# Down projection of an encoder layer: 12 of 22 inner tiles by seven products instead of eight

## The chip, the cores and the metric

The kernel runs on one core of a Trainium2 chip. The metric is the device time of one execution in microseconds. A core has five engines with instruction streams of their own: TensorE (PE; PEld is its weight load), VectorE (DVE), ScalarE (ACT), GpSimd (POOL) and SyncE (SP, which here only starts DMA transfers). They wait for one another by semaphores.

## The reference

One layer of a hybrid encoder on x of 1 x 1024 x 1024 in float32: two token mixers behind a common input projection, their gated sum, and a feed-forward with a gate that is convolved over three positions. D_FF is 2816, which is 22 tiles of 128.

```python
h = _rmsnorm(x, attn_norm_w[layer])
y = _token_mixers(h, w_in[layer], ...)
x = x + jnp.einsum("bsd,de->bse", y, w_out[layer])
h2 = _rmsnorm(x, ffn_norm_w[layer])
x = x + _conv_glu_ffn(h2, ffn_w_up[layer], ffn_dw_w[layer], ffn_dw_b[layer], ffn_w_down[layer])
...
def _conv_glu_ffn(h, w_up, dw_w, dw_b, w_down):
    up = jnp.einsum("bsd,df->bsf", h, w_up)
    gate, val = jnp.split(up, 2, axis=-1)
    gate = _dwconv_centred(gate, dw_w, dw_b)
    return jnp.einsum("bsf,fd->bsd", jax.nn.silu(gate) * val, w_down)
```

The output is the final RMSNorm of x. The change concerns the last product, with `w_down` (2816 x 1024), which is called the down projection here.

## The kernel before

**Numbers in two parts.** Each float32 operand of a large matrix product is split into a high part, rounded to the format that PE multiplies fast (ACT casts it), and a low part, the operand less its high part (DVE subtracts). `split` (L124) does both; both inputs of the subtraction lie in SBUF. `mm3` (L148 to L150) then makes three matmuls: high by high, high by low, low by high. Activations lie transposed, so an output tile is 128 features by 512 positions, half of the sequence, and fills one bank of PSUM. Weights are the stationary operand.

**Ordinary jobs.** `std_job` loads weights for one output tile (`raw_w`, tile `wr`), splits them into two pages `wp`, and accumulates over its inner tiles, for one half of the sequence and then the other. `run_jobs` prepares the next job's weights while one runs. Every two inner tiles a job yields; such a piece is the clock by which `later` schedules chores (loads, splits, gates).

**Seven products.** `pair_job` makes two output tiles and both halves as one 2 x 2 block product in seven products instead of eight, after Winograd. The order is 1, 2, 6, 7, 5, 4, 3. Products 1, 6, 5 and 3 accumulate on one bank (`row`, tag mm), 7 and 4 on another (`col`, tag sc), 2 on a third (tag tr). After 1, 6 and 7 ACT copies the bank into pages `su` (p1, u2, p7; L376); the evacuations to the quadrants (0,0), (1,1), (1,0) and (0,1) follow products 2, 5, 4 and 3. Product 3 starts on the bank that the evacuation of (1,1) reads. The operands are sums and differences of quadrants: the activations' are made once per stage, the weights' sums for each job. In the feed-forward's up projection (22 jobs, four inner tiles per quadrant, 84 matmuls each) the sums of weights are made by DMA transfers that accumulate (`G.dma_start(..., accum_op=ALU.add)`, L301, issued by GpSimd): the column sum `sw`, then two sums into `wr`, each waiting for the one before. The weights of products 1 and 2 (w1/w2) share pages, as do those of 7 and 5 (w7/w5), and of 6 and 3 (w6/w3); w4 stands alone.

**Feed-forward.** `ffn_job(j)` is such a pair job for tile j of the gate and of the value. Its `evac` keeps the value in `ft` pages (L1504) and the gate in `gp`; `gated` runs as a chore during the next job: convolution on ACT and DVE (L1486, L1488), silu, two multiplications on DVE (L1497, L1498), and the store to `d_g` (L1499), which SP issues.

**Down projection.** It goes over the 22 inner tiles in groups of 4, 4, 5, 5 and 4. For a group, `load_g` fetches the two halves of each inner tile into a landing buffer (`ev` or `tm`, seven together), and splits them into pages `hx` or `gx` (48 together). Eight ordinary jobs, one for each output tile, go over the group; the first group's results are copied to `xr` by ACT (L1633), those of the next three are added by DVE (L1639). While a group runs, the next one's operands are loaded, a half every two pieces. The last group runs half after half, adds the residual, transposes, and normalises (L1674, L1675, L1689 and on).

**What sets the order.** PE's order is the program's. The other engines' orders are planned by a scheduler when the kernel is built, with a cost model of its own, except that instructions given to `pin` keep their order; an engine then runs its instructions strictly in the planned order and stands still at the first one that has to wait.

Of the kernel before, what the change touches and what calls it, by code (L numbers as in the profile page):

```python
# [47 lines left out]
def tile_hybrid_encoder(  # L48
# [109 lines left out]
    def later(n, do):  # L158

        chores.append([n, do])  # L160
# [118 lines left out]

        return prep, run  # L280

    def pair_job(src0, src1, nk, acts, wpool, pool, evac, su=4, first=False, late=False, now=False, direct=False, columns=1):

        def steps(w):  # L290
            def both(src, alt, late=late):
                hi, lo = split(w_page(2 * nk, alt), w_page(2 * nk, alt), src, V, late)
                return [(hi[:, :nk], lo[:, :nk]), (hi[:, nk:], lo[:, nk:])]

            def add(o, a):
                if first:
                    V.tensor_tensor(o, o, a, op=ALU.add)
                elif direct:
                    pin(V.tensor_tensor(o, o, a, op=ALU.add))
                else:  # L300
                    G.dma_start(o, a, accum_op=ALU.add)  # L301
# [8 lines left out]
            nc.sync.dma_start(col[:, nk:], src1[:, :nk])  # L310
            if first:
                other = column_page()
                nc.sync.dma_start(other, src1)
                add(col, other)
            elif not direct:
                add(col, src1)
            def sums():
                add(rows[:, :nk], col[:, nk:])
                add(rows[:, nk:], rows[:, :nk])

            def quadrant():
                a22 = pool.tile([P, nk, P], F32, tag="w4", name=nm("w4"), bufs=1)
                nc.sync.dma_start(a22, src1[:, nk:])
                return a22

            if now:
                w[1], w[2] = both(rows, None, False)
                sums()
                yield 0
                w[6], w[3] = both(rows, None, False)  # L330
                yield 1
                a22 = quadrant()
                yield 2
                w[7], w[5] = both(col, pool)
                yield 4
            elif direct:
                yield 2
                other = raw_w(src1, 2 * nk)
                yield 2
                w[1], w[2] = both(rows, None)  # L340
                a22 = quadrant()
                yield 6
                add(col, other)
                sums()
                yield 1
                w[6], w[3] = both(rows, None)
                yield 1
                w[7], w[5] = both(col, pool)
                yield 4
            else:  # L350
                yield 4
                w[1], w[2] = both(rows, None)
                sums()
                a22 = quadrant()
                yield 6
                w[7], w[5] = both(col, pool)
                yield 3
                w[6], w[3] = both(rows, None)
                yield 3
            one = w_page(2 * nk, pool)  # L360
            w[4] = split(one[:, :nk], one[:, nk:], a22, V, late)

        def prep():
            w = Weights(steps)
            return w if late else w.all()

        def run(w):
            def product(i, acc, fresh=True):
                for k in range(nk):
                    mm3(acc, w[i], acts(i)[k], k, fresh and k == 0, k == nk - 1, not fresh)  # L370
                    if k % 2 == 1 or k == nk - 1:
                        yield

            def copy(acc):
                t = page(pool, "su", su)
                A.copy(t, acc)  # L376
# [128 lines left out]
    d_h2 = scratch("d_h2", ND, 2)  # L505
    d_t4 = scratch("d_t4", ND // 2)
    d_g = scratch("d_g", NF, 2)

    def in_cols(c0):
        return w_cols(w_in, 0, ND, c0)  # L510
# [966 lines left out]

    up, gp = Later(), []

    def ffn_job(j):  # L1480
        val = [None, None]

        def gated(hf):
            o, g = hf * H, gp[j % 2]
# [11 lines left out]
            pin(A.activation(c, c, AF.Silu))  # L1496
            V.tensor_tensor(c, c, rstd2[hf], op=ALU.mult)  # L1497
            V.tensor_tensor(val[hf], val[hf], c, op=ALU.mult)  # L1498
            nc.sync.dma_start(d_g[j][hf], val[hf])  # L1499

        def evac(e, half, x0, x1=None, op=None):
            if e == 1:
                val[half] = page(up, "ft", 8)
                V.tensor_tensor(val[half], x0, x1, op=op)  # L1504
                return
            g = gp[j % 2]
# [15 lines left out]
            up,  # L1522
            evac,
            late=True,
            now=j == 0,
            direct=j in (1, 2),
        )

    s_out = Stream(
# [74 lines left out]
    gs, jobs = [], []  # L1604

    def load_g(f, half):

        t = next(landing)()
        nc.sync.dma_start(t, d_g[f][half])
        while len(gs) <= f:  # L1610
            gs.append([None, None])

        def parts():
            gs[f][half] = split(g_page(), g_page(), t, V, True)

        return parts

    s_ffn.fill(14 * (NF - 1) - s_ffn.count)
    for f in range(groups[0]):
        for half in range(2):  # L1620
            later(4, load_g(f, half))
            s_ffn.fill(1)
# [4 lines left out]

    fd = tc.alloc_tile_pool(name="fd", bufs=1, reuse_waits="tile")
    xr = [[page(fd, "xr", 2 * ND) for _ in range(2)] for _ in range(ND)]

    def first_evac(i):
        def f(half, acc):
# [10 lines left out]
    def down_jobs(f0, n, evac):  # L1643
        return [
            std_job(
                w_cols(ffn_w_down, f0 * P, n, i * P), n, lambda k, half: gs[f0 + k][half], evac(i)
            )
            for i in range(ND)
        ]

    def last_jobs(f0, evac):
# [3 lines left out]
        def job(i, half):  # L1655
# [4 lines left out]
                    kept[i] = split(*pages, raw, V)  # L1660
                return kept[i]

            return prep, std_job(None, 4, lambda k, h: gs[f0 + k][h], evac(i), (half,), 1)[1]

        return [job(i, half) for half in range(2) for i in range(ND)]

# [13 lines left out]
    def turn_out(i, half):  # L1680

        t = xr[i][half]
        if i == 0:
            out_sum.append(fd.tile([P, ND, 4], F32, tag="os", name=nm("os"), bufs=2))
            out_y.append(fd.tile([P, 4, D], F32, tag="y", name=nm("y"), bufs=2))
        ss, y = out_sum[half], out_y[half]
        b = bank(next(y_tags))
        for c in range(4):
            T.transpose(b[:, c * P : (c + 1) * P], t[:, c * P : (c + 1) * P], ident)  # L1689
        for c in range(4):  # L1690
            junk = fd.tile([P, P], F32, tag="oj", name=nm("oj"), bufs=2)
            A.activation(
                junk, b[:, c * P : (c + 1) * P], AF.Square, accum_out=ss[:, i, c : c + 1]
            )
        if i == ND - 1:
            rs = cp.tile([P, 4], F32, name=nm("frs"), tag="frs", bufs=2)
# [20 lines left out]
    def scale_out(half, c):  # L1717
# [9 lines left out]
        n = half * 4 + c  # L1727
        nc.sync.dma_start(out[0, n * P : (n + 1) * P, :], y[:, c, :])

    out_sum, out_y, out_r = [], [], []  # L1730
    fnw = fd.tile([P, D], F32, name="fnw")
    f0 = 0
    nc.sync.dma_start(
        fnw, bass.AP(tensor=final_norm_w.tensor, offset=final_norm_w.offset, ap=[[0, P], [1, D]])
    )
    for n, group in enumerate(groups):
        last = n == len(groups) - 1
        if last:
            st = Stream(run_jobs(last_jobs(f0, final_evac)))
            st.fill(4 * ND + 3)  # L1740
            finish(0)
            st.drain()
            advance_chores(1 << 10)
            finish(1)
        else:
            st = Stream(run_jobs(down_jobs(f0, group, add_evac if n else first_evac)))
            st.fill(12)
            for f in range(f0 + group, f0 + group + groups[n + 1]):
                for half in range(2):
                    later(4, load_g(f, half))  # L1750
                    st.fill(2)
            st.drain()
            advance_chores(1 << 10)
        f0 += group
    fd.release()


# [30 lines left out]
```

## Time and profile before

| | |
|---|---|
| median of three runs | 1769.15 us (1767.91 to 1770.44) |
| profiled execution | 1768.21 us, span 1766.4 |
| mean granted PE clock | 0.996 |
| PE busy | 1728.3 us (98%) |
| DVE busy | 1206.5 us (68%) |
| ACT busy | 808.0 us (46%) |
| POOL busy | 158.4 us (9%) |

The span runs from the first to the last instruction of the profiled execution; the time also holds what lies around it. A row of a group of instructions gives line, engine, operation, output and inputs by name, shape and count, then busy time and mean duration in ns, then the idle time before them and what ended it. Rows of the timeline begin with the start and the duration in us. PE's matmuls overlap, so the mean duration of one is longer than the step from one to the next. The feed-forward lies roughly from 1080 to 1510 us of the span, the down projection from there to the end.

### The profile page before, as it was taken

The numbers are of one execution on the slowest core, as the hardware profiler recorded it, in microseconds if no ns is written. First come the engines' busy times: TensorE is split into PE (matmuls) and PEld (weight loads), VectorE is DVE, ScalarE is ACT, GpSimd is POOL, SyncE is SP. The second block draws the span as 40 slices with busy tenths as digits, with TensorE's granted clock in tenths as the row PEclk, the third lists the DMA queues.
The fourth block names the chain that finished last, engine by engine and source line by source line (L and its number), as shares of the span: only waits on it lengthen the run. The fifth ranks groups of instructions, "written<-read, shape, count | busy, mean of one in ns | idle before, by whom it ended". The sixth has DMA issues, their size and how long they took to land.

```text
span 1766.4 us, 30281 instructions
## 1 busy us (share of the span) xinstructions
PE 1728.3 (98%) x11878; PEld 1422.8 (81%) x11878; DVE 1206.5 (68%) x1839; ACT 808.0 (46%) x1518; POOL 158.4 (9%) x171
## 2 busy tenths in 40 slices
PE   8999999999999999999999999999999999999997
PEld 6878888887888787888878888788888888888885
DVE  5599999646688877887365667666676667444455
ACT  7444443334576666776541345333444344422223
POOL 2201111100000000000000002111111111000000
PEclk9999999999999999999999999999999999999998
DMA  8777878856653443435487665677677766534233
GB/s 286 242 166 187 198 176 212 200 143 198 205 184 106 122 123 109 135 113 192 127 259 212 194 207 170 144 161 155 143 146 153 149 138 149 157 103 125 74 92 137
DMA packets 331061, 286.56 MB, mean 162 GB/s; under 512 B 24222, under 2 KB 251302, under 8 KB 330918
## 3 DMA queue, kind: packets, MB, share of 16 engines
q1 hardware_dynamic: 277878, 248.96, 45.2%
q0 software_dynamic: 43824, 34.61, 13.7%
q10 hardware_dynamic: 9216, 1.05, 0.4%
q8 instruction: 93, 1.52, 0.4%
q14 instruction: 50, 0.41, 0.1%
HBM read 189.40 MB, written 76.81 MB: 151 GB/s over the span
## 4 chain that ended last, share of the span: by engine, by line
PE 82%; ACT 5%; DVE 4%; DMA 4%; issue 3%; POOL 1%; ACTq 0%; SPq 0%; POOLq 0%; DVEq 0%
PE mm L148 19%; PE mm L150 19%; PE mm L149 19%; PE sc L148 4%; PE sc L150 4%; PE sc L149 4%; PE ob L1286 2%; PE tr L148 2%; PE tr L150 2%; PE tr L149 2%; PE sc L1113 1%; DMA tm<-d_bm 1%; POOL ors L520 1%; PE sc L1196 1%; DMA sw<-in_ffn_w_up_dram 1%
## 5 line engine op out<-in xcount | busy, mean ns | idle before, releaser
L148 PE MATMUL mm<-hx,wp 128*128 128x512 f32 x1144 | 457.5, 400 | 6.1 <-ACT su L376 2.9
L150 PE MATMUL mm<-hx,wp 128*128 128x512 f32 x1144 | 447.3, 391 | 1.6 <-DVE wp L124 1.6
L149 PE MATMUL mm<-hx,wp 128*128 128x512 f32 x1144 | 446.5, 390 | 0.0
L124 ACT CAST wp<-wr 128x1024 fp32r<-128x1024 f32 (+2 forms) x171 | 162.2, 949 | 341.4 <-PE mm L149 225.5
L148 PEld LDWEIGHTS mm<-hx,wp 128*128 128x128 f32 x1144 | 215.0, 188 | 53.0 <-ACT su L376 3.3
L150 PEld LDWEIGHTS mm<-hx,wp 128*128 128x128 f32 x1144 | 215.0, 188 | 49.8 <-DVE wp L124 3.9
L149 PEld LDWEIGHTS mm<-hx,wp 128*128 128x128 f32 x1144 | 215.4, 188 | 42.2 <-issue 0.7
L124 DVE TENSOR_TENSOR wp<-wr,wp 128x1024 fp32r<-128x1024 f32 (+2 forms) x169 | 186.7, 1105 | 83.0 <-ACT wp L124 78.8
L966 DVE SCALAR_TENSOR_TENSOR acc<-gl,v_b,acc 128x1024 f32<-128x1024 f32 x120 | 150.5, 1306 | 0.4
L1639 DVE TENSOR_TENSOR xr<-mm,xr 128x512 f32<-128x512 f32 x48 | 33.2, 692 | 72.4 <-PE mm L150 72.4
L1062 DVE TENSOR_TENSOR qF<-qF,tb 128x512 f32<-128x512 f32 x96 | 65.4, 689 | 15.5 <-ACT A L1094 14.0
L376 ACT COPY su<-mm 128x512 f32<-128x512 f32 x82 | 47.6, 581 | 61.3 <-PE mm L150 61.1
L124 ACT CAST wq<-sw 128x1024 fp32r<-128x1024 f32 x41 | 43.1, 1051 | 61.7 <-PE mm L149 40.3
L1062 DVE TENSOR_TENSOR kG<-kG,tb 128x512 f32<-128x512 f32 x96 | 65.9, 689 | 5.1 <-PE sc L1196 4.8
L1488 DVE SCALAR_TENSOR_TENSOR tm<-gp,v_a,tm 128x512 f32<-128x512 f32 x88 | 66.1, 751 | 1.9
L148 PE MATMUL mm<-hy,wp 128*128 128x512 f32 x164 | 64.5, 393 | 0.0
L148 PE MATMUL tr<-hx,wp 128*128 128x512 f32 x164 | 64.3, 392 | 0.0
L148 PE MATMUL sc<-hy,wq 128*128 128x512 f32 x164 | 64.2, 392 | 0.0
L149 PE MATMUL mm<-hy,wp 128*128 128x512 f32 x164 | 64.2, 392 | 0.0
L150 PE MATMUL sc<-hy,wq 128*128 128x512 f32 x164 | 64.2, 391 | 0.0
L150 PE MATMUL tr<-hx,wp 128*128 128x512 f32 x164 | 63.8, 389 | 0.0
L149 PE MATMUL tr<-hx,wp 128*128 128x512 f32 x164 | 63.8, 389 | 0.0
(356 smaller groups left out, 3424.2 us busy)
## 6 DMA issues: line engine op xcount, KB each, us to landing
wr<-in_w_in_dram SPq DMA_DIRECT2D x48, 512.0 KB, 5.1
wr<-in_ffn_w_up_dram SPq DMA_DIRECT2D x24, 512.0 KB, 4.0
sw<-in_ffn_w_up_dram SPq DMA_DIRECT2D x44, 256.0 KB, 3.2
d_g<-ft SPq DMA_DIRECT2D x44, 256.0 KB, 3.2
sw<-in_ffn_w_up_dram POOLq DMA_DIRECT2D x20, 512.0 KB, 8.5
sw<-in_w_in_dram SPq DMA_DIRECT2D x38, 256.0 KB
wr<-sw POOLq DMA_DIRECT2D x33, 256.0 KB, 3.4
wr<-wr POOLq DMA_DIRECT2D x33, 256.0 KB, 3.5
```

Source lines behind the costliest of these rows:

```text
L124: parts = A.copy(hi, src), eng.tensor_tensor(lo, src, hi.bitcast(F32), op=ALU.subtract)
L148: T.matmul(acc, whi[:, k, :], ahi, start=first, stop=False, skip_group_check=again)
L149: T.matmul(acc, whi[:, k, :], alo, start=False, stop=False, skip_group_check=again)
L150: T.matmul(acc, wlo[:, k, :], ahi, start=False, stop=last, skip_group_check=again)
L376: A.copy(t, acc)
L520: hold(G.tensor_tensor(dst, dst, mhalf.to_broadcast(list(dst.shape)), op=ALU.pow))
L966: V.scalar_tensor_tensor(acc, g[:, k : k + S], tap(k), acc, op0=ALU.mult, op1=ALU.add)
L1062: V.tensor_tensor(o, a, b, op=op)
L1113: T.matmul(b[g, o], A_t[:, at : at + 32], Q_t(at), start=True, stop=True)
L1286: T.matmul(o[:, sl], l, r, start=(n == 0), stop=(n == len(terms) - 1))
L1488: V.scalar_tensor_tensor(c, g[:, o + k : o + k + H], vec("fdw", k * NF + j), c, op0=ALU.mult, op1=ALU.add,)
L1639: V.tensor_tensor(xr[i][half], acc, xr[i][half], op=ALU.add)
```

## The change

Twelve inner tiles, 6 to 17, go through the down projection as two groups of six by `pair_job`: three inner tiles per quadrant, output tiles i and i + 4 as a pair, four jobs of 63 matmuls per group. Tiles 0 to 5 form one ordinary group before them, 18 to 21 the last group, as before. Three things go with it.

- The operands. The feed-forward takes tiles 6 to 17 in pairs (f, f + 3). After the gate of the second tile of a pair, `g_sums` makes three differences and one sum on DVE, out of `ft` pages, and SP stores them to `d_gc`. One half of the first tile of each pair is no longer stored, as nothing reads it. `load_seven` fetches and splits 21 operand tiles per group into the same 48 pages: 12 for the first seven-product group while the ordinary group runs, 9 when its pages come free; for the second group three early and 18 around the last job of the first.
- The weights. `pair_job` gets a third way of making sums (`sums_on`): two plain loads, `sr` and `so`, two buffers each; w1/w2 split from `sr`; then four additions on GpSimd, two into `sw` and two in place into `sr`; then the splits of w7/w5, w6/w3 and w4.
- The evacuations. `seven_evac` adds to `xr`: for three of four quadrants GpSimd first adds `xr` to, or subtracts it from, the SBUF page (p1, u2, p7), and DVE combines that with the bank; the fourth is one DVE addition.

In the planned order GpSimd does for each pair job: the addition to p1, the four sums for the next job, and among or after the last of them the additions to u2 and p7.

The pools are laid out anew: `fs` holds the new stage's tiles (`sr`, `so`, `sw`, `wq`, `su`), and the output pages `y` come after it in `fy`. Up to the end of the feed-forward, each engine's planned order is that of before but for the new subtractions and stores.

```diff
+            if sums_on is not None:
+                rows, other = (
+                    wpool.tile([P, 2 * nk, P], F32, tag=tag, name=nm(tag), bufs=2)
+                    for tag in ("sr", "so")
+                )
+                nc.sync.dma_start(rows, src0)
+                nc.sync.dma_start(other, src1)
+                r0, r1, o0, o1 = rows[:, :nk], rows[:, nk:], other[:, :nk], other[:, nk:]
+                yield 4
+                w[1], w[2] = both(rows, None)
+                col = wpool.tile([P, 2 * nk, P], F32, tag="sw", name=nm("sw"), bufs=columns)
+                for o, a, b in (
+                    (col[:, :nk], r0, o0), (col[:, nk:], o0, o1), (r0, r0, col[:, nk:]), (r1, r1, r0)
+                ):
+                    pin(sums_on.tensor_tensor(o, a, b, op=ALU.add))
+                yield 6
+                w[7], w[5] = both(col, pool)
+                yield 3
+                w[6], w[3] = both(rows, None)
+                yield 3
+                one = w_page(2 * nk, pool)
+                w[4] = split(one[:, :nk], one[:, nk:], o1, V, late)
+                return
...
+    def g_sums(f, b11, b12, b21, b22):
+        def less(a, b):
+            o = page(up, "ft", 8)
+            V.tensor_tensor(o, a, b, op=ALU.subtract)
+            return o
+
+        t7 = less(b12, b22)
+        nc.sync.dma_start(d_gc[f][3], t7)
+        t6 = less(t7, b11)
+        nc.sync.dma_start(d_gc[f][2], t6)
+        t5 = less(b11, b12)
+        nc.sync.dma_start(d_gc[f][1], t5)
+        t4 = page(up, "ft", 8)
+        V.tensor_tensor(t4, t6, b21, op=ALU.add)
+        nc.sync.dma_start(d_gc[f][0], t4)
...
-            nc.sync.dma_start(d_g[j][hf], val[hf])
+            if not (hf and j in b12_only):
+                nc.sync.dma_start(d_g[j][hf], val[hf])
+            if hf and FIRST <= j < LAST0:
+                kept_g.append((j, *val))
+                if len(kept_g) == 2:
+                    (f, b11, b12), (_, b21, b22) = kept_g
+                    kept_g.clear()
+                    g_sums(f, b11, b12, b21, b22)
...
-    groups = [4, 4, 5, 5, 4]
+    def load_seven(f0, i, k):
+        f = f0 + k
+        src = {1: d_g[f][0], 2: d_g[f + NS][0], 3: d_g[f + NS][1]}
+        return load_part((f0, i, k), src[i] if i < 4 else d_gc[f][i - 4])
...
-    def add_evac(i):
-        def f(half, acc):
-            V.tensor_tensor(xr[i][half], acc, xr[i][half], op=ALU.add)
+    def seven_evac(i):
+        def f(e, half, x0, x1=None, op=None):
+            t = xr[i + e * ND // 2][half]
+            if x1 is None:
+                V.tensor_tensor(t, x0, t, op=ALU.add)
+                return
+            if (e, half) == (1, 1):
+                G.tensor_tensor(x0, x0, t, op=ALU.add)
+            else:
+                G.tensor_tensor(x1, x1, t, op=op)
+            V.tensor_tensor(t, x0, x1, op=op)
...
+    for s in range(SEVENS):
+        todo = [(FIRST + 2 * NS * s, i, k) for i in PRODUCTS for k in range(NS)]
+        if s == 0:
+            at = [12 + 2 * n for n in range(12)] + [starts[0] - 2 + n for n in range(9)]
...
+            at = [starts[s] - 36 + 6 * n for n in range(NS)]
+            at += [
+                starts[s] - per_seven - 2 + per_seven // 7 * n + max(0, k - 1)
+                for n in range(1, 7)
+                for k in range(NS)
+            ]
+        for n, key in zip(at, todo):
+            fill_to(n)
+            later(4, load_seven(*key))
```

More of the change, by code (lines that the diff above doesn't have):

```diff
@@ L280, in duo_job, with pair_job @@
         return prep, run
-    def pair_job(src0, src1, nk, acts, wpool, pool, evac, su=4, first=False, late=False, now=False, direct=False, columns=1):
+    def pair_job(src0, src1, nk, acts, wpool, pool, evac, su=4, first=False, late=False, now=False, direct=False, columns=1, sums_on=None):
         def steps(w):
@@ L1600, in g_page, with load_part, parts @@
         return hx() if next(n_g) == 0 else page(fd, "gx", 16, F32R)
-    groups = [4, 4, 5, 5, 4]
     landing = itertools.cycle([ev] * 3 + [tmp] * 4)
-    gs, jobs = [], []
-    def load_g(f, half):
[L1608 to L1616, printed above, removed]
+    gs = {}
+    def load_part(key, src):
+        t = next(landing)()
+        nc.sync.dma_start(t, src)
+        def parts():
+            gs[key] = split(g_page(), g_page(), t, V, True)
+        return parts
+    def load_g(f, half):
+        return load_part((f, half), d_g[f][half])
+    def load_seven(f0, i, k):
+        f = f0 + k
+        src = {1: d_g[f][0], 2: d_g[f + NS][0], 3: d_g[f + NS][1]}
+        return load_part((f0, i, k), src[i] if i < 4 else d_gc[f][i - 4])
     s_ffn.fill(14 * (NF - 1) - s_ffn.count)
-    for f in range(groups[0]):
+    for f in range(FIRST):
         for half in range(2):
@@ L1728, in scale_out @@
         nc.sync.dma_start(out[0, n * P : (n + 1) * P, :], y[:, c, :])
[L1730 to L1744, printed above, removed]
-        else:
[L1746 to L1754, printed above, removed]
+    out_y, out_r = [], []
@@ new lines, in tile_hybrid_encoder, with fill_to @@
+    per_std, per_seven = 2 * ((FIRST + 1) // 2), 7 * ((NS + 1) // 2)
+    jobs = std_down(0, FIRST, first_evac)
+    first_seven = seven_down(FIRST)[0]
+    starts = [ND * per_std]
+    for s in range(SEVENS):
+        jobs += seven_down(FIRST + 2 * NS * s)
+        if s == 0:
+            jobs[ND] = (lambda: ahead[0], first_seven[1])
+        starts.append(starts[-1] + ND // 2 * per_seven)
+    st = Stream(run_jobs(jobs, 1))
+    ahead = [None]
+    def fill_to(n):
+        while st.count < n:
+            st.fill(1)
+            if st.count == starts[0] - 2 * per_std + 2:
+                ahead[0] = first_seven[0]()
+            elif ahead[0] is not None and st.count < starts[0] - per_std + 2:
+                ahead[0].tick()
@@ L1755, in tile_hybrid_encoder @@
+    n = starts[-1] - per_seven - 12
+    for f in range(LAST0, NF):
+        for half in range(2):
+            fill_to(n)
+            later(4, load_g(f, half))
+            n += 3
+    st.drain()
+    advance_chores(1 << 10)
+    fs.release()
+    fy = tc.alloc_tile_pool(name="fy", bufs=1, reuse_waits="tile")
+    st = Stream(run_jobs(last_jobs(LAST0, final_evac)))
+    st.fill(4 * ND + 3)
+    finish(0)
+    st.drain()
+    advance_chores(1 << 10)
+    finish(1)
+    fy.release()
     fd.release()
```

58 lines of the change are left out of this document (45 added, 13 removed).

## The prediction

> **What bounds the kernel now.** I read the page first, then a table by stretches, then who waited for whom on PE, then the down projection and one feed-forward job in time.
>
> ```profile
> span 1766.4 us, 30281 instructions
> PE 1728.3 (98%) x11878; PEld 1422.8 (81%) x11878; DVE 1206.5 (68%) x1839; ACT 808.0 (46%) x1518; POOL 158.4 (9%) x171
> ...
> 1170.00:1400.00 230.00, 230.00 (x1004) 188.22 (x1003) 156.17 (x204) 93.61 (x132) 39.36 (x36) 1.00 0.70 149
> 1520.00:1700.00 180.00, 180.00 (x796) 149.10 (x795) 80.01 (x120) 48.05 (x82) 0.00 (x0) 1.00 0.34 103
> ...
> PE mm L150 <- DVE wp L124: 1.6, 3, 0.6
> ```
>
> The two middle lines are a stretch of the feed-forward and one of the down projection (length, then busy time and count of PE, PEld, DVE, ACT, POOL, then granted clock, DMA share, GB/s). PE never rests in either, so a matmul taken away is time gained, but at its pace and not at the 390 ns that the page gives for one: 180/796 = 0.226 us in the down projection, 230/1004 = 0.229 in the feed-forward. DVE has room in the down projection (80 of 180 us) and little in the feed-forward (156 of 230). GpSimd does nothing at all in the down projection. The last line says that in the whole run PE waited for split weights three times, 1.6 us together: what feeds it comes in time, so every later feed has to be looked at against its margin.
>
> **What goes.** Twelve inner tiles cost 12 x 8 outputs x 2 halves x 3 = 576 matmuls; as two groups of seven products they cost 2 x 4 x 7 x 3 x 3 = 504. The built program has 72 fewer: 72 x 0.226 = **-16.3 us**.
>
> **Pace of the products.** The other seven-product stage at hand, the feed-forward, runs at 0.229. At that pace the 504 matmuls lose 504 x 0.003 = 1.5 us, at the pace of the down projection nothing. I take **+0.5**, bounds 0 and 1.5.
>
> **Feed-forward: four more subtractions in six jobs.** In the built order the four stand on DVE directly ahead of the evacuation of quadrant (1,1), after the last multiply of the gate; product 3 accumulates on the bank which that evacuation reads.
>
> ```profile
> 1398.39 0.69 DVE L1511 TENSOR_TENSOR gp<-gp,rs 128x512 f32<-128x512 f32 x1
> 1398.99 0.69 DVE L1498 TENSOR_TENSOR ft<-ft,tm 128x512 f32<-128x512 f32 x1
> 1399.60 1.22 DVE L124 TENSOR_TENSOR wp<-wr,wp 128x1024 fp32r<-128x1024 f32 x1
> ...
> 1403.86 0.69 DVE L1498 TENSOR_TENSOR ft<-ft,tm 128x512 f32<-128x512 f32 x1
> 1404.30 0.39 PE L150 MATMUL mm<-hx,wq 128*128 128x512 f32 x1
> 1404.73 0.69 DVE L1504 TENSOR_TENSOR ft<-su,mm 128x512 f32<-128x512 f32 x1 [0.17 <-PE mm L150]
> 1407.29 0.39 PE L148 MATMUL mm<-hy,wp 128*128 128x512 f32 x1
> ...
> 1424.64 0.69 DVE L1498 TENSOR_TENSOR ft<-ft,tm 128x512 f32<-128x512 f32 x1
> 1425.25 0.68 DVE L1504 TENSOR_TENSOR ft<-su,mm 128x512 f32<-128x512 f32 x1
> 1426.83 0.39 PE L148 MATMUL mm<-hy,wp 128*128 128x512 f32 x1
> ```
>
> One after the other, such instructions follow at 0.61 us (first three lines). So the evacuation starts no sooner than 1404.55 + 4 x 0.61 = 1406.99, ends at 1407.68, and product 3, which began at 1407.29, begins some 0.45 later. In the next job the evacuation began at 1425.25; 2.44 later it would end at 1428.4, 1.6 after product 3 was due (1426.83). I take 0.6 each: **+3.6**, bounds 2.7 and 10.
>
> The weights' sums of the feed-forward are a chain of transfers, and its slack is gone in some jobs:
>
> ```profile
> d_g<-ft SPq DMA_DIRECT2D x44, 256.0 KB, 3.2
> sw<-in_ffn_w_up_dram POOLq DMA_DIRECT2D x20, 512.0 KB, 8.5
> ...
> 1408.63 0.50 SPq L310 DMA_DIRECT2D sw<-in_ffn_w_up_dram  x1
> ...
> 1414.27 1.56 POOL L301 DMA_DIRECT2D sw<-in_ffn_w_up_dram  x1 [5.06 <-DMA sw<-in_ffn_w_up_dram]
> ...
> 1413.67 1.05 ACT L124 CAST wp<-wr 128x1024 fp32r<-128x1024 f32 x1 [8.08 <-DMA wr<-wr]
> ...
> 1414.75 1.23 DVE L124 TENSOR_TENSOR wp<-wr,wp 128x1024 fp32r<-128x1024 f32 x1 [3.83 <-ACT wp L124]
> ```
>
> The four new stores (256 KB each) stand on SP ahead of the next loads of sw, and these also wait for the split that now follows the delayed evacuation: 2 us later, behind 1 MB, of which the stretch above moves 149 GB/s on average. The split at 1414.75 is w6/w3, needed from about 1415.5, so a chain that is later by some us shows on PE. I take 0.3 for each of six jobs, **+2.0** rounded up, bounds 0 and 9.
>
> **The new stage: GpSimd and DVE share a way to memory.** No row has a 384-wide GpSimd addition, but nearby ones price it:
>
> ```profile
> 41.36 1.28 POOL L124 TENSOR_TENSOR hx<-ev,hx 128x512 fp32r<-128x512 f32 x1 [9.98 <-ACT hx L124]
> 42.02 0.69 DVE L784 TENSOR_TENSOR gl<-mm,tm 128x512 f32<-128x512 f32 x1 [1.39 <-PE mm L150]
> ...
> 49.58 1.22 DVE L124 TENSOR_TENSOR wp<-wr,wp 128x1024 fp32r<-128x1024 f32 x1
> 50.40 1.55 POOL L124 TENSOR_TENSOR hx<-ev,hx 128x512 fp32r<-128x512 f32 x1 [1.99 <-ACT hx L124]
> ...
> 1084.22 1.04 POOL L548 TENSOR_TENSOR tm<-ident,r 128x512 f32<-128x512 f32 x1
> 1084.46 1.95 DVE L124 TENSOR_TENSOR hy<-ft,hy 128x512 fp32r<-128x512 f32 x2 [1.22 <-ACT hy L124]
> ...
> L124 DVE TENSOR_TENSOR wp<-wr,wp 128x640 fp32r<-128x640 f32 x16 | 13.1, 817 | 0.0
> L124 DVE TENSOR_TENSOR hx<-tm,hx 128x512 fp32r<-128x512 f32 x18 | 12.0, 687 | 4.1 <-ACT hx L124 4.1
> L376 ACT COPY su<-mm 128x512 f32<-128x512 f32 x24 | 13.8, 576 | 16.5 <-PE mm L150 16.5
> L124 ACT CAST wp<-wr 128x640 fp32r<-128x640 f32 x16 | 11.7, 732 | 78.1 <-PE mm L149 78.1
> L124 ACT CAST hx<-tm 128x512 fp32r<-128x512 f32 x18 | 10.5, 617 | 2.1 <-DMA tm<-d_g 2.1
> ```
>
> A GpSimd addition of 512 columns takes 1.28 us, and a DVE instruction with one operand in PSUM runs beside it undisturbed (first two lines). A DVE split, both of whose inputs lie in SBUF, does not: the addition at 50.40 ends at 51.95, 1.15 after the split that ended at 50.80; and the two splits at 1084.46 end at 1086.41, so the first ended at 1085.80, 0.54 after GpSimd's end at 1085.26. They take turns, and the one that waited has all but some 0.15 us still to do. Scaled by columns: an addition of 384 takes 1.0 alone and 0.87 after a wait; a split of 768 takes 0.95 and 0.8, of 384 0.56 and 0.41, of 512 0.69 and 0.54. A DVE evacuation costs 0.69, a copy on ACT 0.58, and a reader of PE starts 0.04 after the last matmul's end (1404.30 + 0.39 to 1404.73).
>
> A pair job has 63 matmuls, products of 2.04 us, 14.3 in all. In the built order GpSimd does in each: the addition to p1, four sums for the next job, the additions to u2 and to p7; only then can DVE evacuate (1,1), on which product 3 waits, due at 12.24. By itself DVE has 3 x 0.95 + 0.56 + 4 x 0.69 = 6.2 us per job and ACT less, so it is the order that costs. A quiet job, from its first matmul: p1 is copied at 2.25 to 2.83 and added by 4.2; w4's split, ready at 3.3, waits and ends at 4.6; sum 1 at 5.5; the split of w1/w2 6.3 (sum 3 overwrites what it reads); sums 2, 3, 4 at 7.2, 8.2, 9.2; u2 10.5; p7 11.8; evacuation 12.5: product 3 is 0.3 late. Each operand split that stands in between adds about 0.45. Five jobs lie between the changes of group: two have one such split, one two, one none, and the last has no sums to make: 4 x 0.3 + 4 x 0.45 = **+3.0**, bounds 0 and 10.
>
> The changes of group. At the first (standard to seven), six of nine operand splits and w6/w3's stand ahead of that evacuation. From 2.9 on the shared way has to carry additions 1.28 + 2 x 1.15, sums 4 x 0.87, splits 6 x 0.54 + 0.8 + 0.8 + 0.41 = 12.3; the evacuation ends at 15.2 + 0.7 = 15.9 instead of 12.2: **+3.7**. At the second, 18 operand pairs are split within two jobs, eight of them ahead of the evacuation: 1.28 + 2.3 + 3.5 + 0.41 + 0.8 + 8 x 0.57 = 12.8, so its end is at 16.4: +4.2, and the next job begins at 18.5. Behind it stand seven operand splits, two evacuations and two splits of weights, the last of them w6/w3: 9 x 0.61 + 0.87 + 0.95 = 7.3 after 16.4, and the next job's first addition and one or two sums (1.2 to 2.6) between: 24.9 to 26.3, where product 6 is due at 22.6: +3.0; its own evacuation adds 0.5. Together **+7.7**. Bounds for both, 3 (at the second ACT casts w6/w3 behind p1's copy and an operand: 2.83 + 0.62 + 0.85, then DVE's 0.95, makes 5.2 against 4.08) and 18. The third change has no sums, and eight pairs over two jobs: 0.
>
> That both inputs in SBUF make the turns, the Trainium skill has as a rule too ("SBUF — State Buffer", section "Who interferes with whom"), but there the one that comes second stands still for the whole of the other and then has all of its own to do. The rows have 0.15 us less, the sum goes by the rows, and what the rule would make of it is rival three.
>
> **What is hidden.** The first group's 12 operand pairs (8 before) take DVE 12 x 0.61 = 7.3 us behind the last feed-forward job; by the built order the twelfth is ready when the first standard job, 36 matmuls or 8.1 us long, reaches it, and the standard jobs' DVE is then more than half idle, as in the stretch from 1520. Operand loads, two a job and more at the changes, find seven landing buffers and 34% of DMA in use there. Each of these, uncovered, would cost its 0.61 per pair or its transfer time once.
>
> **Sum.** -16.3 + 0.5 + 3.6 + 2.0 + 3.0 + 3.7 + 7.7 = +4.2. The profiled execution took 1768.2 (span 1766.4 and 1.8 around it), 0.9 under the median of the runs, 1769.15. So 1772.4 for such an execution, and **1773.3** against the median: what PE saves is given back at hand-overs.
>
> **Rivals.**
> One, faster: the turns rarely meet. If DVE, which can run ahead, has its splits done while GpSimd waits for copies, p7's addition ends by 11.4 in a job and product 3 never waits; that is the point where it turns. For it speaks the pair at 41.36 and 42.02, against it the built order, which puts the sums between p1's and p7's additions in every job. Then the stage costs 0.5 + 2.5 (ACT's order), the feed-forward 3.6 + 1: -16.3 + 0.5 + 3.0 + 4.6 = -8.2, so 1761. Chance 0.25.
> Two, slower: the feed-forward's chain of sums is late by 2 us in all six jobs behind the stores, 10 more than I took: 1783. For it, the split at 1414.75; against it, the job between two such jobs can catch up. Chance 0.15.
> Three, slower: the one that waits has its whole 1.28 or 0.69 still to do, 0.14 more at every hand-over, some 15 at each of two changes of group and 9 in each of five jobs: 75 x 0.14 = 10.5 more, 1784. Against it, the 1.15 and 0.54 above. Chance 0.08. (This is the rule of the Trainium skill's "SBUF — State Buffer" as it is written.)
> That PE's work does not shrink is ruled out by the built order.
>
> **How the numbers follow.** A run can tell about 0.2%, 3.5 us, from no change: 1765.6 to 1772.7. The forecast has 0.52, of which I put 0.05 below that band, 0.18 in it, 0.29 above; its own range is 1766 to 1781. Rival one gives 0.20 faster and 0.05 same, the others 0.23 slower. Faster 0.25, same 0.23, slower 0.52. The range from 1760 to 1785 takes in rivals one to three at their own values and leaves out what lies beyond: the high ends of all bounds at once.
>
> **What would show it.** PE's waits in the new stage name ACT wp/DVE wp (w6/w3) and, at product 3, the evacuation; POOL additions between splits show 1.4 to 1.9 us instead of 1.28. In the feed-forward, six jobs have a gap of 0.4 to 1.7 before product 3. I am wrong if the span from the first pair job to the last is near 8 x 14.3 = 114 us (then rival one), or if the feed-forward lengthens by over 10 us (two).

## The result and the profile after

The changed kernel takes **1776.22 us** (median of 5 runs, 1773.60 to 1779.20) against 1769.15 before: a ratio of **1.0043, interval 1.0029 to 1.0057**. It is slower, by 7 us; 1773.3 was forecast, with a range of 1760 to 1785. The profiled execution took 1773.6 us, the shortest of the five and 5.4 more than the one of before.

First the page of the changed kernel:

```profile
span 1771.8 us, 30408 instructions
PE 1720.7 (97%) x11806; PEld 1410.2 (80%) x11806; DVE 1254.6 (71%) x1873; ACT 839.9 (47%) x1568; POOL 233.8 (13%) x227
```

PE has 72 matmuls less and is busy 7.6 us less, and yet the span is 5.4 us longer. Next its table by stretches: length, then busy time and count of PE, PEld, DVE, ACT, POOL, then granted clock, DMA share, GB/s.

```profile
1509.00:1575.00 66.00, 66.00 (x293) 54.66 (x292) 25.92 (x34) 25.74 (x44) 4.46 (x4) 1.00 0.52 154
1575.00:1590.70 15.70, 13.09 (x54) 9.27 (x52) 13.31 (x13) 9.33 (x17) 9.96 (x7) 1.00 0.47 137
1590.70:1635.00 44.30, 43.09 (x188) 35.01 (x189) 29.77 (x33) 19.37 (x32) 25.68 (x20) 1.00 0.39 113
1635.00:1660.00 25.00, 19.38 (x69) 14.78 (x68) 20.68 (x25) 10.38 (x17) 12.75 (x9) 0.86 0.65 188
...
1640.00:1643.80 3.80, 3.80 (x11) 3.00 (x10) 3.80 (x7) 0.64 (x2) 0.00 (x0) 0.55 0.85 272
```

The six standard tiles (first line) run without a rest, as the whole stage did before. PE rests from the first change of group on: 2.6 us in the second line, 1.2 in the third, 5.6 in the fourth. The fourth has something else: its clock is 0.86, and 0.55 in the last line, a part of it in which PE is always busy and yet has only 11 matmuls in 3.8 us.

Who waited for whom on PE (total, times, longest):

```profile
PE mm L148 <- DVE xr L1716: 7.0, 6, 4.0
...
PE mm L148 <- DVE ft L1562: 2.9, 6, 0.7
PE mm L150 <- DVE wp L124: 2.8, 4, 1.6
...
PE tr L1781 <- DVE xr L1768: 1.6, 2, 0.9
...
PE sc L149 <- DVE hx L124: 1.4, 2, 0.7
```

All but the third row are new. The first is product 3 of the pair jobs waiting for the evacuation of quadrant (1,1), the second the same in the feed-forward, the third split weights (1.6 before), the fourth the end of the kernel, the last the split operands of product 4 at the first change of group.

One feed-forward job in time, where the differences stand ahead of that evacuation:

```profile
1405.09 2.02 DVE L1517 TENSOR_TENSOR ft<-ft,ft 128x512 f32<-128x512 f32 x3
...
1407.03 0.68 DVE L1527 TENSOR_TENSOR ft<-ft,ft 128x512 f32<-128x512 f32 x1
...
1407.56 0.39 PE L150 MATMUL sc<-hy,wq 128*128 128x512 f32 x1
1407.63 0.68 DVE L1562 TENSOR_TENSOR ft<-su,mm 128x512 f32<-128x512 f32 x1
...
1408.36 0.50 PE L148 MATMUL mm<-hy,wp 128*128 128x512 f32 x1 [0.41 <-DVE ft L1562]
```

Product 4's last matmul starts at 1407.56, and the next should follow 0.23 later; it comes at 1408.36, behind the evacuation: 0.57 beyond the step. The six such jobs have 0.85, 0.58, 0.73, 0.58, 0.57 and 0.58.

A quiet pair job, in which GpSimd's queue is the late one:

```profile
1613.50 1.73 POOL L317 TENSOR_TENSOR sw<-so 128x384 f32<-128x384 f32 x1
...
1615.31 1.01 POOL L317 TENSOR_TENSOR sr<-sr,sw 128x384 f32<-128x384 f32 x1
1615.52 1.35 DVE L124 TENSOR_TENSOR hx<-ev,hx 128x512 fp32r<-128x512 f32 x1 [1.16 <-ACT hx L124]
1616.40 1.35 POOL L317 TENSOR_TENSOR sr<-sr 128x384 f32<-128x384 f32 x1
1617.71 1.29 POOL L1715 TENSOR_TENSOR su<-su,xr 128x512 f32<-128x512 f32 x1
1618.97 1.28 POOL L1713 TENSOR_TENSOR su<-su,xr 128x512 f32<-128x512 f32 x1
1620.28 0.69 DVE L1716 TENSOR_TENSOR xr<-su,mm 128x512 f32<-128x512 f32 x1 [3.41 <-POOL su L1713]
...
1621.03 0.50 PE L148 MATMUL mm<-hx,wp 128*128 128x512 f32 x1 [0.56 <-DVE xr L1716]
```

The turns are there: a sum of 384 columns takes 1.01 alone and 1.35 or 1.73 with a DVE split at its side, a split of 512 takes 1.35 instead of 0.69. DVE itself is idle for 3.41 us ahead of the evacuation: it waits for p7's addition, the last of GpSimd's seven instructions in a job.

The second change of group, on PE, DVE and GpSimd:

```profile
1633.49 3.19 DVE L124 TENSOR_TENSOR gx<-tm,gx 128x512 fp32r<-128x512 f32 x2
1634.69 1.44 POOL L317 TENSOR_TENSOR sr<-sr 128x384 f32<-128x384 f32 x1
...
1635.21 0.39 PE L150 MATMUL sc<-hx,wq 128*128 128x512 f32 x1
...
1636.09 1.71 POOL L1713 TENSOR_TENSOR su<-su,xr 128x512 f32<-128x512 f32 x1
1636.61 2.35 DVE L124 TENSOR_TENSOR gx<-ev,gx 128x512 fp32r<-128x512 f32 x2
1638.88 0.67 DVE L1716 TENSOR_TENSOR xr<-su,mm 128x512 f32<-128x512 f32 x1
...
1639.61 0.50 PE L148 MATMUL mm<-hx,wp 128*128 128x512 f32 x1 [4.01 <-DVE xr L1716]
...
1640.58 0.63 PE L148 MATMUL mm<-hx,wp 128*128 128x512 f32 x1
1641.01 0.63 PE L149 MATMUL mm<-hx,wp 128*128 128x512 f32 x1
...
1649.87 0.50 PE L150 MATMUL mm<-hx,wp 128*128 128x512 f32 x1 [1.61 <-DVE wp L124]
```

Splits and additions in turns, then the evacuation, and product 3 is 4.17 us late. One microsecond after PE goes on, its matmuls follow at 0.43 instead of 0.227, eight times. A second pause, for w6/w3, is 1.78 long and is followed by eight more such steps.

### The profile page after: what moved, and what is told of

It is laid out like the page before. It is cut to its first block, busy times and chain, and to the rows that moved or that the text cites. A ratio compares the mean times of both kernels' runs of the same rounds, so it can differ in the third digit from the quotient of the medians.

```text
span 1771.8 us, 30408 instructions
## 1 busy us (share of the span) xinstructions
PE 1720.7 (97%) x11806; PEld 1410.2 (80%) x11806; DVE 1254.6 (71%) x1873; ACT 839.9 (47%) x1568; POOL 233.8 (13%) x227
## 3 DMA queue, kind: packets, MB, share of 16 engines
q10 hardware_dynamic: 9216, 1.05, 0.4%
## 4 chain that ended last, share of the span: by engine, by line
PE 68%; DMA 8%; DVE 7%; ACT 6%; issue 6%; POOL 4%; ACTq 0%; SPq 0%; POOLq 0%; DVEq 0%
PE mm L148 16%; PE mm L149 15%; PE mm L150 15%; PE sc L148 3%; PE sc L150 3%; PE sc L149 3%; DMA sw<-in_ffn_w_up_dram 3%; PE ob L1311 2%; PE tr L150 2%; PE tr L148 2%; PE tr L149 2%; DMA wr<-wr 1%; PE sc L1138 1%; DVE wp L124 1%; POOL sr L317 1%
## 5 line engine op out<-in xcount | busy, mean ns | idle before, releaser
L148 PE MATMUL mm<-hx,wp 128*128 128x512 f32 x1068 | 429.6, 402 | 12.3 <-DVE xr L1716 7.0
L150 PE MATMUL mm<-hx,wp 128*128 128x512 f32 x1068 | 418.7, 392 | 2.5 <-DVE wp L124 2.4
L149 PE MATMUL mm<-hx,wp 128*128 128x512 f32 x1068 | 417.6, 391 | 0.0
L148 PEld LDWEIGHTS mm<-hx,wp 128*128 128x128 f32 x1068 | 201.4, 189 | 58.5 <-DVE xr L1716 8.6
L150 PEld LDWEIGHTS mm<-hx,wp 128*128 128x128 f32 x1068 | 201.1, 188 | 48.2 <-DVE wp L124 4.9
L149 PEld LDWEIGHTS mm<-hx,wp 128*128 128x128 f32 x1068 | 201.7, 189 | 39.5 <-issue 0.7
L124 DVE TENSOR_TENSOR wp<-wr,wp 128x1024 fp32r<-128x1024 f32 (+2 forms) x145 | 169.8, 1171 | 83.7 <-ACT wp L124 73.6
L124 ACT CAST wq<-sw 128x1024 fp32r<-128x1024 f32 (+1 forms) x49 | 49.8, 1016 | 67.2 <-PE mm L149 41.9
L301 POOL DMA_DIRECT2D wr<-sw x33 | 29.2, 885 | 340.2 <-DVE wp L124 203.4
L148 PE MATMUL tr<-hx,wp 128*128 128x512 f32 x180 | 70.5, 392 | 0.0
L150 PE MATMUL tr<-hx,wp 128*128 128x512 f32 x180 | 70.1, 389 | 0.0
L149 PE MATMUL tr<-hx,wp 128*128 128x512 f32 x180 | 70.0, 389 | 0.0
L148 PE MATMUL mm<-hy,wp 128*128 128x512 f32 x164 | 65.1, 397 | 2.9 <-DVE ft L1562 2.9
L400 ACT COPY su<-sc 128x512 f32<-128x512 f32 x49 | 28.9, 589 | 79.6 <-PE sc L150 79.6
L124 DVE TENSOR_TENSOR wq<-sw,wq 128x1024 fp32r<-128x1024 f32 (+1 forms) x49 | 57.9, 1182 | 11.7 <-ACT wq L124 11.4
L148 PE MATMUL sc<-hy,wq 128*128 128x512 f32 x164 | 64.2, 392 | 0.0
```

What stands on the lines that cost most here:

```text
L124: parts = A.copy(hi, src), eng.tensor_tensor(lo, src, hi.bitcast(F32), op=ALU.subtract)
L148: T.matmul(acc, whi[:, k, :], ahi, start=first, stop=False, skip_group_check=again)
L149: T.matmul(acc, whi[:, k, :], alo, start=False, stop=False, skip_group_check=again)
L150: T.matmul(acc, wlo[:, k, :], ahi, start=False, stop=last, skip_group_check=again)
```

## The experiments

Each is compared with runs of the kernel before on its own chip. "Gain" is the ratio of the change (1.0043) less that of the experiment, times 1768 us. The ratios have intervals of 0.0009 to 0.0014 either way, so a gain is uncertain by some 3 us (an estimate from the two intervals). A trace is of one execution only, which can lie some us from the median.

**1. Bank first.** DVE adds the bank to the residual at once, and GpSimd adds the other page afterwards, so that no GpSimd work stands ahead of the evacuation.

```
-                G.tensor_tensor(x0, x0, t, op=ALU.add)
+                V.tensor_tensor(t, t, x1, op=op)
+                G.tensor_tensor(t, t, x0, op=ALU.add)
...
-                G.tensor_tensor(x1, x1, t, op=op)
-            V.tensor_tensor(t, x0, x1, op=op)
+                V.tensor_tensor(t, x0, t, op=ALU.add)
+                G.tensor_tensor(t, t, x1, op=op)
```

> DVE evacuates the bank into xr at once, and GpSimd adds the page (p1, u2, p7) to xr afterwards; the count of operations is that of the change. If PE's waits in the new stage come from DVE standing before quadrant (1,1) for GpSimd's last addition, and from splits and additions taking turns: the quiet jobs lose their 0.4 to 1.2 us ahead of product 3 altogether, the first change of group falls from 3.9 to about 2.2, the first wait of the second from 4.2 to about 2.6 (its eight operand splits still take turns with sums) and, if the half pace after it comes from the length of the pause, that goes too: together about 9 us under the change, near 1767. If instead DVE's own load at the changes of group is what PE waits for, only the quiet jobs gain, 3 us: 1773.

Measured: 1769.89, ratio 1.0009 (0.9999 to 1.0018), a gain of 6.0. A quiet job now, on DVE and GpSimd:

```profile
1619.36 1.01 POOL L317 TENSOR_TENSOR sr<-sr,sw 128x384 f32<-128x384 f32 x1
1620.25 0.69 DVE L1713 TENSOR_TENSOR xr<-xr,mm 128x512 f32<-128x512 f32 x1 [1.84 <-PE mm L150]
1620.44 1.01 POOL L317 TENSOR_TENSOR sr<-sr 128x384 f32<-128x384 f32 x1
```

The evacuation (L1713 here) waits for PE alone, with GpSimd's sums still running, and the pauses of the quiet jobs are gone. Who waited for that evacuation:

```profile
PE mm L148 <- DVE xr L1713: 3.4, 2, 2.8
```

Two waits instead of six, and nearly all of it is at the second change, a pause of 2.96 us. The place of GpSimd's additions ahead of the evacuation is what the quiet jobs paid for. The gain lies between the two expectations, 1767 and 1773: the pause at the second change fell less than expected (to 2.96, where 2.6 was expected), and six half-pace steps still follow it.

**2. Late differences.** The four differences of the feed-forward go six steps later, behind the evacuation.

```
-                    g_sums(f, b11, b12, b21, b22)
+                    later(6, lambda: g_sums(f, b11, b12, b21, b22))
```

> The four subtractions of a pair are called one piece after quadrant (1,1) is evacuated instead of directly ahead of it; nothing else. If the six gaps ahead of product 3 in the feed-forward (0.57 to 0.85 us each) come from that place in DVE's order, they go, and the feed-forward shortens by 4 us: near 1772. If they come from DVE being full in the feed-forward as a whole, the wait moves to another product or to the splits of weights (w6/w3), and the time stays near 1776.

Measured: 1772.58, ratio 1.0023 (1.0009 to 1.0036), a gain of 3.5. The row of waits on L1562 is gone, and the six pauses with it (3.9 us). In their place product 6 starts late three times (0.95, 0.62 and 0.39), which the trace puts down to ACT's copy of p1. That copy stands behind the cast of w6/w3, which waits for the chain of sums: part of what the rival expected. At the first change of group the pauses are those of the changed kernel, but here eight half-pace steps follow them. The waits in the pair jobs are as they were:

```profile
PE mm L148 <- DVE xr L1716: 7.1, 6, 4.0
```

**3. Sums that only write.** Each of the four sums of weights is left out, and two fills with zero stand in its place.

```
-                    pin(sums_on.tensor_tensor(o, a, b, op=ALU.add))
+                    pin(sums_on.memset(o, 0.0))
+                    pin(sums_on.memset(o, 0.0))
```

> Leaves out the weights' sums: each of GpSimd's four sums becomes two fills with zero of the same page, so that GpSimd has about as much to do, in the same places and behind the same waits on DVE's split, but reads nothing. If GpSimd's reads and DVE's splits of two SBUF inputs exclude one another: the splits beside them take their own 0.69 and 0.95 us, product 3 is on time in the quiet jobs, and the first wait of the second change falls from 4.2 to under 1.5 us. If GpSimd is simply late because of what it waits for, and the long rows (1.3 to 1.7 us) come from elsewhere, product 3 is as late as in the change.

Measured, in one run: 1764.11, where the runs of the kernel before on that chip had a median of 1767.87. Of the waits on product 3:

```profile
PE mm L148 <- DVE xr L1717: 2.0, 2, 1.4
```

(L1717 is L1716, one line down.) The quiet jobs have no pause, the first change 0.54 and 0.76, the second 1.52 and 1.38 and no half pace. A split beside the fills takes its own time:

```profile
1599.33 0.42 POOL L317 MEMSET sw<- 128x384 f32 x1
...
1599.49 0.94 DVE L124 TENSOR_TENSOR wp<-sr,wp 128x768 fp32r<-128x768 f32 x1
```

In the changed kernel the same split took 1.17 beside a sum. So GpSimd instructions that only write make no turns here. One run can't give an interval, but the places of the pauses say what the sums cost, in time and in turns together: most of the 7.0. The two can't be told apart here, since the two fills also take less than a sum, 0.84 from one pair to the next against 1.01.

**4. Sums on DVE.**

```
-                sums_on=G,
+                sums_on=V,
```

> The four sums of weights are made by DVE instead of GpSimd; the additions to p1, u2 and p7 stay on GpSimd. If turns cost the time: a sum costs DVE 0.41 to 0.56 instead of a hand-over of 0.87, p7's addition is done by 10.5 in a quiet job and product 3 is on time; the changes of group lose about 2 us each: 6 to 8 us under the change, near 1769. If DVE's load sets the time at the changes of group, they get longer by 4 sums of 0.5 each, and the whole stays near 1776.

Measured: 1772.41, ratio 1.0024 (1.0010 to 1.0038), a gain of 3.4. From its waits:

```profile
PE mm L150 <- DVE wp L124: 2.9, 3, 2.0
PE mm L148 <- ACT wp L124: 2.5, 2, 1.7
...
PE mm L148 <- DVE xr L1716: 1.5, 1, 1.5
```

The evacuation's wait shrinks from 7.0 to 1.5. At the second change w6/w3 are late instead, 1.86 for ACT's cast and 2.13 for DVE's split, again with half pace behind. The time lies between the two expectations, 1769 and 1776: the turns go, and DVE's longer queue takes part of it back.

**5. Edits 1 and 2 together.**

> The two edits of the earlier runs together: DVE adds the bank to the residual first and GpSimd the other page behind it, and the feed-forward's four differences are put six steps later, behind the evacuation. They act in different stages, so if each pause is what the theory says (a queue position ahead of product 3's evacuation), the gains add: 1776.2 - 6.3 - 3.6 = 1766.3 us, ratio to the kernel before 0.999, with the six feed-forward gaps and the quiet jobs' gaps both gone and the second change of group left (3 + 1 us and a stretch of half pace). The rival, that PE is held by something common to the whole run (DVE's load, the transfers), expects no more than the better of the two alone: 1769.9, ratio 1.001.

Measured: 1768.67, ratio 1.0000 (0.9988 to 1.0012), a gain of 7.6 where 9.5 would be their sum. By time alone that doesn't exclude the rival, whose 1.0009 lies in the interval. The trace speaks for the theory: both sets of pauses are gone. Product 3's one large pause here:

```profile
1628.78 0.39 PE L150 MATMUL sc<-hx,wq 128*128 128x512 f32 x1
1631.96 0.50 PE L148 MATMUL mm<-hx,wp 128*128 128x512 f32 x1 [2.79 <-DVE xr L1713]
1632.29 0.39 PE L149 MATMUL mm<-hx,wp 128*128 128x512 f32 x1
```

It is as long as in run 1 (2.95 against 2.96), but here no half pace follows. The profiled execution took 1762.34, 6.3 less than the median of its twelve, so its length says little of the others.

**6. And the sums on DVE.** Runs 5 and 4 together.

> The same two edits and the weights' sums on DVE, so that GpSimd keeps only its additions to the residual, which are now behind the evacuation and off PE's way. If the turns with GpSimd are what is left at the changes of group, what remains is about 1.5 us at the first change, 3.5 at the second without half pace, 2 in the feed-forward and 2.3 in the tail: 1767.9 - 16.3 + 9.3 = 1761 us, ratio 0.996. The rival, that DVE's own queue is too long at the changes of group (its splits of operands and weights, whoever makes the sums), expects the four sums per job (0.5 us each) to lengthen it: w6/w3 late by some 2 to 4 us at both changes with half pace behind, 1766 to 1769, ratio 0.999 to 1.001.

Measured: 1767.25, ratio 0.9995 (0.9983 to 1.0007): the rival's time. At the second change w6/w3 is late, 1.96 for ACT's cast and 2.97 for DVE's split, with 12 half-pace steps behind. With the sums off GpSimd, what PE waits for there is split weights out of ACT's and DVE's own queues.

**7. Operands spread.** Run 5, with the operand splits at both changes spread: from four steps earlier at the first, over 18 steps instead of 12 at the second.

```
-  [12 + 2 * n for n in range(12)] + [starts[0] - 2 + n for n in range(9)]
+  [12 + 2 * n for n in range(12)] + [starts[0] - 6 + 4 * n // 3 for n in range(9)]
...
-  starts[s] - per_seven - 2 + per_seven // 7 * n + max(0, k - 1)
+  starts[s] - per_seven - 2 + 3 * n + k - 1
```

> Bank first and late differences as before, and the operand splits of the two changes of group spread: at the first change they begin four steps earlier and take eleven steps instead of nine, at the second the 18 come one a step over 18 steps instead of 12. Theory (the pauses at the changes come from splits that stand on DVE and in turns with GpSimd's sums ahead of the evacuation): at the second change six splits instead of nine stand ahead of it, 3 x 0.6 to 0.9 = 1.8 to 2.7 us less of the 2.95 there, and at the first change operand waits of 1.5 us go; without them no half pace. From 1768.7 to some 1762 us, ratio 0.9965. Rival (what the changes need is simply too much for the two engines, wherever it stands): the pause moves into the next job's w6/w3 and evacuation, the total stays near 5 us and the time at 1768, ratio 1.000.

Measured: 1766.71, ratio 0.9988 (0.9975 to 1.0001), between the two expectations and not clear of run 5. In the profiled run the second change costs 2.6 us instead of 5.4. At the first the waits of 0.86, 0.62, 0.73 and 0.52 have become one of 2.02 ahead of product 3, and eight half-pace steps follow it. At the second change product 3's pause, which was to lose 1.8 to 2.7 us, fell only from 2.95 to 2.36; what went is the wait for w6/w3, from 2.45 to 0.23.

**8. Operands spread, sums on DVE, and the last pair job's additions on DVE.**

> As the run before it in this batch, with the weights' sums on DVE and the additions of the very last pair job on DVE as well, so that GpSimd adds only in seven jobs, behind evacuations. Theory: the tail's 1.35 us before the last weights' split goes (a DVE split of 0.68 there took 1.78 beside GpSimd's addition), the changes of group keep about 2 us in all; 1761 us, ratio 0.996. Rival (DVE's own queue is too long at the changes): w6/w3 late by 3 to 5 us with half pace behind, 1766, ratio 0.999.

Measured: **1764.43, ratio 0.9968 (0.9955 to 0.9981)**: faster than both kernels. Its page:

```profile
PE 1719.6 (98%) x11806; PEld 1411.0 (80%) x11806; DVE 1260.8 (72%) x1908; ACT 839.5 (48%) x1568; POOL 195.7 (11%) x192
```

Its waits in the stages of the change:

```profile
PE mm L150 <- DVE wp L124: 2.1, 3, 1.3
PE mm L149 <- DVE hx L124: 2.0, 2, 1.3
...
PE mm L150 <- DVE hx L124: 1.3, 1, 1.3
PE mm L148 <- DVE xr L1713: 1.3, 1, 1.3
```

The first change costs 0.85, the second three waits of 1.4, without half pace. The time lies between the two expectations, 1761 and 1766. The changes of group keep 5.1 us where the theory had 2, and the tail's wait for the last weights' split (L150 on hx, 1.35 in runs 5 to 7) stays, though GpSimd no longer works there. DVE's own queue of evacuations and additions stands ahead of it.

## Why the prediction held, and where it was off

Pauses are counted beyond the step of 0.2267 us, in the profiled execution.

- **72 matmuls less, -16.3:** held, 11878 to 11806. **Pace, +0.5:** products run at 2.04 us for nine, the pace of the stage before; 0.
- **Feed-forward, differences, +3.6:** 3.9 for the six pauses, each with some 0.11 of restart behind. Run 2 takes them away.
- **Feed-forward, chain of sums, +2.0:** 0.8, in one job at 1475, where product 6 waits for p1's copy and ACT had the late cast of w6/w3 ahead of it. The step that failed is "I take 0.3 for each of six jobs": the job between two such jobs catches up, as the prediction had against rival two.
- **Quiet jobs, +3.0:** 0.81, 0.72, 0.40, 1.19 and 0: 3.1. Runs 1 and 3 take them away, each in its own way.
- **First change, +3.7:** 3.4 in all, but by another route. Only 0.72 of it is a late product 3; before that PE waits for the splits of w6/w3 (0.53), of w4 (0.44) and of two of product 4's operands (0.85, 0.90). The amount of shared work was right: the evacuation of (1,1) ends 16.0 after the job's first matmul (1574.49 to 1590.52), where 15.9 was forecast. The place where it shows was not.
- **Second change, +7.7:** 4.17 (forecast 4.2) and 1.78 (forecast 3.0 + 0.5), and 16 steps at half pace, 3.2, which the prediction had not: 9.2.
- **Third change, 0:** 2.2 in the last jobs behind it (0.26, 0.90, 1.05). The step that failed is the cover of the loads: DVE works in order, and its evacuations there stand behind instructions that wait for transfers, at 1717 for the last weights by way of ACT's cast, at 1750 for the saved residual. Rows of DVE and ACT ahead of these two pauses:

```profile
1716.56 0.62 ACT L124 CAST gx<-wr 128x512 fp32r<-128x512 f32 x1 [1.43 <-DMA wr<-in_ffn_w_down_dram]
1717.21 0.69 DVE L124 TENSOR_TENSOR gx<-wr,gx 128x512 fp32r<-128x512 f32 x1 [1.23 <-ACT gx L124]
1717.82 0.69 DVE L1768 TENSOR_TENSOR xr<-mm,tm 128x512 f32<-128x512 f32 x1
...
1750.24 0.69 DVE L1767 TENSOR_TENSOR tm<-tm,xr 128x512 f32<-128x512 f32 x1 [2.46 <-DMA tm<-d_x]
```

These waits differ from run to run (0.28 and 0.45 in run 2), and why the transfers come later than before was not tried.

That makes -16.3 + 3.9 + 0.8 + 3.1 + 3.4 + 9.2 + 2.2 = +6.3, and with some 0.1 of restart behind each of twenty pauses +8.3. Set side by side, the two profiled executions give +8.1 from 1160 us to the end, 5.2 of it in the feed-forward. The executions differ by only 5.4, since the part before that took 2.8 less in the one after: 0.6 by 1080 us, and 2.1 at a pause near 1140 that both kernels have, 2.47 at full pace against 3.05 with half pace behind. Here too ACT's cast of w6/w3 waits for the chain of sums; the prediction, which read 1.6 us as all of PE's waits for split weights, left that out. This pause is between 1.36 and 3.43 in the ten profiled executions, whatever the kernel, so it moves single times by some us. The medians differ by 7.1.

So the mechanism held, queues ahead of an evacuation and turns, but that the time came within 3 us is in part luck. The wait for w6/w3 at the second change was put at 3.5 and cost 1.78, and the chain of sums 2.0 and cost 0.8; against that, half pace (3.2), the last jobs (2.2) and the restarts (some 2) stood in no term.

Rival one (turns rarely meet, 1761) fell: turns are in every job that makes sums, and the eight pair jobs take 131.6 us (1574.49 to 1706.08) where 114 would have spoken for it. Run 1 takes the additions out of product 3's way by another order, and gave 6.0. Rival two fell with the 0.8. Rival three would have put 45 x 0.14 = 6.3 of its 10.5 us on the quiet jobs, beyond 3.0; they cost 3.1, as the sum with 0.15 less at each hand-over had it. Its rule, in the Trainium skill's "SBUF — State Buffer", section "Who interferes with whom", has the second instruction fully blocked while the first has its ports; in the quiet job above a split that takes 0.69 ends 0.55 after the sum it waited for (1616.87 against 1616.32), so 0.14 of it was done by then.

## What to carry to other kernels

Fewer matmuls pay only as far as what feeds and empties the banks keeps its place: cost every new instruction by what it is queued ahead of, not by its engine's load (GpSimd was busy 13% of the span, and the last of its seven instructions in a job decided). Where an evacuation needs a sum of a bank and a page, take the bank first on the engine that is free and add the page behind it; that needed no instruction more and gave most of the loss back. Where groups change, try the new operands' splits spread over both jobs (in the trace of run 7 that halved the second change's pauses and moved the first's; its median is not clear of run 5), and reckon that a pause of some 2 us on PE can cost as much again in matmuls at half pace.

## What the runs showed of the hardware

**Half pace.** After some pauses matmuls of 512 columns follow at 0.43 us instead of 0.227, for 6 to 12 steps, with a granted clock of 0.50 to 0.55 over such a stretch. In the changed kernel and runs 1 and 7 it came behind pauses of 4.17, 2.96 and 2.02 us, and behind 1.78 us which followed another pause by 8 us. It did not come behind 2.95 and 2.45 us in run 5, nor behind 2.36 in run 7. In run 2 eight such steps came at the first change (1590.07 to 1593.43, clock 0.51), behind pauses of only 0.44, 0.85, 0.90 and 0.73 within 5 us; the changed kernel has the same four pauses there and goes on at full pace. The kernel before has it too, near 1145 us (granted clock over 4.6 us there):

```profile
1144.00:1148.60 4.60, 4.56 (x14) 3.39 (x13) 4.47 (x8) 2.98 (x6) 0.17 (x1) 0.63 0.97 132
```

At that place the pause was 3.05 to 3.43 in the five traces where half pace followed and 1.36 to 2.47 in the five where it didn't. But by the pauses above, the length of a single one doesn't decide it. The Trainium skill ("TensorE: Matmul & The Clock Gate", Part 1) has a clock that halves after an idle window of about 3.4 us that runs freely, so that, by our reading, the place of a pause in the window counts; a figure of 426.7 ns for the cold step there agrees with 0.43. That pauses under 3.4 us brought it on here is not in that rule as it reads, unless a window that is partly idle counts. The short pauses of run 2 would fit that; no run here shows it.

**A GpSimd instruction can be kept out for long.** In run 6 an addition of 1.29 us alone is shown with 6.54 us while DVE's splits and sums stood back to back:

```profile
1644.40 6.54 POOL L1717 TENSOR_TENSOR xr<-xr,su 128x512 f32<-128x512 f32 x1 [5.77 <-DVE xr L1716]
```

In the changed kernel the two took turns one by one. Spans on GpSimd are rough, and why DVE kept its place here and not there was not tried.
